# One encoder layer on one core: conditioning loads one pair of steps earlier, fewer conditioning steps beside the combination, and the fourth kind's softmax division done by the transposing product

## The chip, the core and the metric

The kernel runs on one core of a Trainium2 chip. The metric is the device time of one execution in microseconds (us), lower is better. Times, spans and waits below are from the runs of the kernel before and from the profile of one of its executions. Engines are named as the profile names them: PE is TensorE (PEld its weight loads), DVE is VectorE, ACT is ScalarE, POOL is GpSimd, SP is SyncE, which only issues transfers here.

## What is computed

One layer of an encoder trunk, for 1024 tokens of width 1024, all in float32. A conditioning vector c of width 1024 gives six modulation vectors; the layer is two residual blocks. The first has two attention branches: neighbourhood attention with 8 heads, and a mixture of three dilated windows with 4 heads each whose outputs are combined by their softmax denominators.

```python
mod = c_act @ w_ada[l] + b_ada[l]
sh1, sc1, gt1, sh2, sc2, gt2 = jnp.split(mod, 6, axis=-1)
h = rms_norm(x, g_norm1[l]) * (1.0 + sc1) + sh1
proj = h @ w_in[l]
qa, ka, va, qb, kb, vb, gates = jnp.split(proj, split_at, axis=-1)
o_a = neighbourhood_attention(rms_norm(qa), rms_norm(ka), va, rpb[l])
# three dilated windows on qb, kb, vb, combined by softmax of their log denominators
o_b = jnp.einsum('gbsh,gbshd->bshd', wts, jnp.stack(outs, axis=0))
merged = gate_a * (o_a @ w_proj_a[l]) + gate_b * (o_b @ w_proj_b[l])
x = x + gt1 * (merged @ w_o[l])
h2 = rms_norm(x, g_norm2[l]) * (1.0 + sc2) + sh2
a, up = jnp.split(h2 @ w_ffn_in[l], 2, axis=-1)
x = x + gt2 * ((jax.nn.silu(a) * up) @ w_ffn_out[l])
```

Inside `neighbourhood_attention` the scores get a bias, go through a softmax over at most 384 keys here, and the probabilities P multiply v.

## The kernel before

Every large product is made of three products of a high and a low part (`PASS`), so PE has most of the work. The program has these stages, by the time of the profiled execution: x is normalised and turned, and the first six blocks of tokens are projected (0 to 62 us); the combined projection with the attention worked in between (62 to 527); the first gate products with the last attention (527 to 616); the other gates, the merge, the output projection and the feed-forward part (616 to the end).

The projection is a loop over `n` from 6 to 91. `n = 8u + t`: `u` is one of ten units (a pair of heads: six of the dilated kinds 0, 1 and 2, then four of kind 3, the neighbourhood attention, which is "the fourth kind"), and `t` is a block of 128 tokens. Each `n` has eight chunks of three projection products on PE (line 305); between the fourth and the fifth chunk stand the scores of one item of attention, the product of P and v of an older one (line 510), the turns of q and k (line 370), and the turn of P of the item before (line 495). From `n = 58` on the items are those of kind 3, one for each `n`, until `n = 89`. An item of kind 3 has 128 queries, 2 heads and three blocks of 128 keys; the first and the last of a unit have two blocks.

For a head of kind 3, `at_qk` adds the bias to the scores and finds the negative maximum on DVE (line 483), takes the exponential and its sum on ACT (line 484), the reciprocal of the sum on DVE (line 486), and multiplies P by it on DVE (line 487). `at_turn`, one `n` later, transposes the blocks of P on PE into a PSUM bank with tag `t` (line 495) and copies the bank to SBUF, on ACT for the first head and on DVE for the second (lines 501 and 499). There are two banks of each tag.

The conditioning vectors that are needed late (4096 columns) are worked out beside all this: `ada_step` (line 278) is called once for an `n`, 65 times. A step multiplies a 128 by 512 piece of `w_ada` by one column of the activated c and adds it to `acc` on DVE (lines 292 and 294). The pieces are loaded in pairs, 512 KB at a time, by the step that uses the first of the pair (line 288), into a tile `wa` of the pool tag `big`. After eight steps `ada_row` (line 269) sums over the partitions with a product on PE into a bank `t` (line 271), adds the bias and stores the row; its two small tiles are of the tag `raw`.

`big` has eight tiles of 4 KB for a partition. They also hold v of a unit, the biases `rb` of kind 3, the pieces `tp`, the combination's sum `oacc` and more. `raw` has six tiles, into which all weights are loaded before they are split; the combination's `ut` and `fb` use them too. The combination of the three dilated kinds (`combine_step`) runs from `n = 64` (`COMB`) on: it turns the factors `fb` on PE into a bank `t` (line 665), and multiplies and adds on DVE (lines 673 to 676).

The order on PE is the order of the program. On DVE, ACT, POOL and SP a scheduler chooses the order when the program is built: it simulates the program and takes the first instruction in the program's order whose inputs are there by its simulation. In the built program each engine then runs its list strictly in order, so that an instruction that waits holds up all that stand behind it on its engine.

Of the kernel before, what the change touches and what calls it, by code (L numbers as in the profile page):

```python
# [10 lines left out]
F32 = mybir.dt.float32  # L11
F32R = mybir.dt.float32r
AF = mybir.ActivationFunctionType
ALU = mybir.AluOpType

S = 1024
# [7 lines left out]
NRAW, NHL = 6, 10  # L24
# [12 lines left out]
PAIRED, RBT, COMB = 58, 5, 64  # L37
# [6 lines left out]
def hybrid_layer(ctx: ExitStack, tc: tile.TileContext, x, colp, wada1, wada2, bada2, wqkv, wg, wpa, wpb,  # L44
                 wo, w1, w2, hgain, ropeg, rope, rbias, bmask, g2r, out):
    nc = tc.nc

    def pool(name, side, **kw):
        return tc.alloc_tile_pool(name=name, bufs=1, side=side, reuse_waits="tile", **kw)
# [4 lines left out]
    wp = pool("w", "left")  # L54
# [20 lines left out]
    def bank(tag):  # L75
        return ps.tile([128, 512], F32, tag=tag, name="ps_" + tag)
# [9 lines left out]
    ident = const.tile([128, 128], F32, name="ident")  # L86
# [5 lines left out]
    for i in (0, 2):  # L92
        nc.vector.scalar_tensor_tensor(hg[:, i:i + 1], hg[:, i:i + 1], 0.125, hg[:, i + 1:i + 2],
                                       op0=ALU.mult, op1=ALU.mult)
# [56 lines left out]
    def big(name, shape=None, dtype=F32):  # L151
        return ap_.tile(shape or wide, dtype, tag="big", bufs=NBIG, name=name)
# [27 lines left out]
    def unit_load(u, k):  # L180
        return wload(wqkv[u, :, k, :], 384)
# [84 lines left out]
    ada_state = {"i": 0}  # L266
    ada_acc = {}

    def ada_row(c):
        pm = bank("t")  # L270
        nc.tensor.matmul(pm[0:1, :], ones, ada_acc[c], start=True, stop=True)
        row = wp.tile([1, 512], F32, tag="raw", bufs=NRAW, name="row")
        br = wp.tile([1, 512], F32, tag="raw", bufs=NRAW, name="brow")
        nc.sync.dma_start(br, bada2[:, c * 512:(c + 1) * 512])
        nc.vector.tensor_add(row, pm[0:1, :], br)
        nc.sync.dma_start(mod_d[c * 512:(c + 1) * 512].rearrange("(o n) -> o n", o=1), row)

    def ada_step():
        i = ada_state["i"]
        ada_state["i"] += 1  # L280
        c, kk = divmod(i, 8)
        if kk == 0 and c > 0:
            ada_row(c - 1)
        if i >= 64:
            return
        if kk % 2 == 0:
            ada_acc["w"] = big("wa2", [128, 2, 512])
            nc.sync.dma_start(ada_acc["w"], wada2[c, :, kk:kk + 2, :])
        wa = ada_acc["w"][:, kk % 2, :]
        if kk == 0:  # L290
            ada_acc[c] = ap_.tile([128, 512], F32, tag="acc2", bufs=1, name="acc2")
            nc.vector.tensor_scalar(ada_acc[c], wa, cact[:, 0:1], None, op0=ALU.mult)
        else:
            nc.vector.scalar_tensor_tensor(ada_acc[c], wa, cact[:, kk:kk + 1], ada_acc[c],  # L294
                                           op0=ALU.mult, op1=ALU.add)
# [176 lines left out]
    @urgent(AQ)  # L472
    def at_qk(I, h):
        U, nq = I.U, I.nq
        nk = I.nkb * 128
        pS = I.pS[h]
        P = I.P[h] = ap_.tile([128, 512], F32, tag="p", bufs=4, name="P")
        if U.kind < 3:
            nm, sm = U.st[:nq, I.item, h:h + 1], U.st[:nq, I.item, 2 + h:3 + h]
        else:  # L480
            sx = ap_.tile([128, 3], F32, tag="sx", bufs=4, name="sx")
            nm, sm = sx[:nq, 0:1], sx[:nq, 1:2]
        nc.vector.tensor_tensor_reduce(P[:nq, :nk], pS[:nq, :nk], I.masks[h], -1.0, 3.0e38, ALU.add, ALU.min, nm)  # L483
        nc.scalar.activation(P[:nq, :nk], P[:nq, :nk], AF.Exp, scale=-1.0, bias=nm, accum_out=sm)  # L484
        if U.kind == 3:
            nc.vector.reciprocal(sx[:nq, 2:3], sm)
            nc.vector.tensor_scalar(P[:nq, :nk], P[:nq, :nk], sx[:nq, 2:3], None, op0=ALU.mult)

    @urgent(AT)
    def at_turn(I, h):  # L490
        nq, nkb = I.nq, I.nkb
        P = I.P[h]
        pt = bank("t")
        for i in range(nkb):
            nc.tensor.transpose(pt[:, i * 128:i * 128 + nq], P[:nq, i * 128:(i + 1) * 128], ident[:nq, :nq])
        PT = I.PT[h] = ap_.tile([128, 4, 128], F32, tag="pT", bufs=4, name="PT")
        src = pt.rearrange("p (b q) -> p b q", q=128)[:, :nkb, :nq]
        if h:
            nc.vector.tensor_copy(PT[:, :nkb, :nq], src)
        else:  # L500
            nc.scalar.activation(PT[:, :nkb, :nq], src, AF.Copy)
# [413 lines left out]
    for n in range(6, 92):  # L915
        u, t = divmod(n, 8)
        if u < 10:
            if t == 0:
                units.append(new_unit(u, [nextw[u, k] for k in range(KT)]))
            U = units[u]  # L920
            chunks = [lambda k=k, U=U, t=t: proj_chunk(U, t, k) for k in range(KT)]
        elif n - 80 < NPRE:
            chunks = gate_pre(n - 80)
        else:
            chunks = []
        if u + 1 < 10:
            for k in ([0, 1, 2, 3, 4, 5, 6, 7] if n == 6 else [t] if u else []):
                raws[u + 1, k] = unit_load(u + 1, k)
            if t == 6:
                for k in range(2):  # L930
                    nextw[u + 1, k] = wsplit(raws[u + 1, k])
        if t == 2 and 1 <= u <= 10:
            for slot, I in unit_items(units[u - 1]):
                if I.U.kind < 3:
                    waiting.append(I)
                else:
                    ready.setdefault(8 * u + 2 + slot, []).append(I)
        if n == 8 * 7 + 5:
            combine_stats()
        ci = n - COMB  # L940
        if 0 <= ci < 12:
            combine_prep(ci)
        if n >= PAIRED:
            done, prev, cur = prev, cur, ready.pop(n, [])
        elif n % 2:
            done, prev, cur = prev, cur, []
            if waiting:
                cur = [Cluster()]
                while waiting and cur[0].keys + waiting[0].nkb * 128 <= 512:
                    cur[0].add(waiting.pop(0))  # L950
        else:
            done = []

        def chunk():
            if chunks:
                chunks.pop(0)()
                k = 8 - len(chunks)
                if t == 7 and u + 1 < 10 and k < 8 and k >= 2:
                    nextw[u + 1, k] = wsplit(raws[u + 1, k], nc.vector if k % 2 else None)

        turns = [(units[0], tt) for tt in {8: (0, 1), 9: (2, 3), 11: (4, 5), 13: (6, 7)}.get(n, ())]
        if PAIRED <= n <= 81 or 9 < n < PAIRED and n % 2:
            turns += [(units[m // 8], m % 8) for m in ((n - 2,) if n >= PAIRED else (n - 3, n - 2)) if m >= 8]
        chunk()
        chunk()
        chunk()
        chunk()
        if n < 10:
            while chunks:
                chunk()  # L970
        if n >= PAIRED or n % 2 or n < 10:
            for I in cur:
                if I.__class__ is Cluster:
                    cl_scores(I)
                    cl_qk(I)
                else:
                    at_scores(I)
                    at_qk(I, 0)
                    at_qk(I, 1)
            for I in done:  # L980
                (cl_pv if I.__class__ is Cluster else at_pv)(I)
            for j in range(0, len(turns), 2):
                qk_turns(turns[j:j + 2], "s" if n < 10 else "v")
            for I in prev:
                if I.__class__ is Cluster:
                    cl_turn(I)
                else:
                    at_turn(I, 0)
                    at_turn(I, 1)
        chunk()  # L990
        chunk()
        chunk()
        chunk()
        if n >= 8 and (t != 7 or u > 8) and ada_state["i"] < 65:
            ada_step()
        if 2 <= u < 6 and t < 5:
            if t in (2, 4):
                t_piece(2 * (u - 2) + t // 2 - 1, 2)
            if t in (0, 2):
                t_piece(2 * (u - 2) + t // 2, 0)  # L1000
            if t in (1, 3):
                t_piece(2 * (u - 2) + t // 2, 1)
        if n in (85, 88):
            w1_combos((n - 85) // 3, EARLY[(n - 85) // 3])
        if 1 <= ci < 13:
            combine_step(ci - 1)
        while chunks:
            chunk()
        if u < 10:
            proj_post(U, t)  # L1010
            if U.kind == 3 and t == RBT:
                bias_tabs(U)
# [240 lines left out]
    for t in range(8):  # L1253
        pbs = [bank("dsv"[t % 3]) for _ in range(2)]
        ko = KFIRST if t == 0 else (KLAST if t == 7 else range(KT))
        for n, k in enumerate(ko):
            for hf in range(2):
                for a, b in PASS:
                    nc.tensor.matmul(pbs[hf], h2T[a][:, k, t * 128:(t + 1) * 128], wow[hf, k][b],  # L1259
                                     start=(n == 0 and (a, b) == PASS[0]), stop=(n == KT - 1 and (a, b) == PASS[2]))  # L1260
# [398 lines left out]
```

## Time and profile before

| | us |
|---|---|
| median of 3 runs | 1508.05 |
| lowest and highest run | 1505.69, 1510.28 |
| the profiled execution's own time | 1513.64 |
| its span, first to last instruction | 1511.8 |
| mean granted clock of TensorE | 0.997 of full speed |

The profile is read from the busy shares to the waits. An engine that is busy nearly all the time is a candidate for the bound; its idle time, and who ended it, tells what else costs time. A row of the list of waits reads: who waited, for whom, us in total, times, longest. A row of the timeline reads: start, length, engine, line, operation, result and inputs, size, count, and in brackets the idle time of the engine just before and what ended it. The records of PE overlap, because products are pipelined: the time that a product costs is read from the distance of two starts, not from the length of a record. A float32 product that is no transposition has two records.

### The profile page before, as it was taken

What the parts mean: (1) busy time and instruction counts of PE and PEld (TensorE: products, weight loads), DVE (VectorE), ACT (ScalarE), POOL (GpSimd) and SP (SyncE); (2) the same over time, 40 slices, a digit from 0 to 9 for tenths busy, and PEclk for the clock granted to TensorE, in tenths of its full rate; (3) what the DMA queues carried; (4) which work ended last, traced back from release to release, by engine and by line L of the source; (5) the groups of instructions that cost most, each with busy time, mean ns of one, the idle gap of its engine ahead of it and who ended that gap; (6) DMA issues with size and microseconds to landing.
All of it is one profiled execution on the core that took longest, in us unless ns stands there. A gap on an engine that the chain in (4) does not pass through costs nothing.

```text
span 1511.8 us, 24199 instructions
## 1 busy us (share of the span) xinstructions
PE 1486.6 (98%) x8156; PEld 1266.7 (84%) x8156; DVE 1087.9 (72%) x2265; ACT 669.9 (44%) x1691; POOL 535.6 (35%) x540
## 2 busy tenths in 40 slices
PE   8999999999999999999999999999999999999998
PEld 7999989998888877788888888888888888887886
DVE  6868777767888744466665497788767777599468
ACT  5656656555645554245532344233222333344442
POOL 0432333221100040001351311677767776104464
PEclk9999999999999999999999999999999999999999
DMA  9626444645235164833553235335433334798343
GB/s 365 232 80 190 144 145 145 190 137 166 76 114 176 47 192 135 308 106 123 176 178 143 87 96 182 119 132 180 157 130 105 109 108 146 269 366 288 99 150 103
DMA packets 150637, 241.65 MB, mean 160 GB/s; under 512 B 26464, under 2 KB 69088, under 8 KB 149744
## 3 DMA queue, kind: packets, MB, share of 16 engines
q1 hardware_dynamic: 131936, 226.45, 45.7%
q10 hardware_dynamic: 18576, 13.64, 2.8%
q8 instruction: 65, 1.06, 0.3%
q14 instruction: 60, 0.49, 0.1%
HBM read 179.89 MB, written 60.15 MB: 159 GB/s over the span
## 4 chain that ended last, share of the span: by engine, by line
PE 79%; DMA 8%; DVE 7%; ACT 3%; issue 2%; POOL 1%; SPq 0%; ACTq 0%; DVEq 0%
PE ps_d L305 11%; PE ps_v L1324 7%; PE ps_d L1324 7%; PE ps_s L1324 7%; PE ps_t L1324 6%; PE ps_d L705 4%; PE ps_s L1494 3%; PE ps_d L1494 3%; DMA wa<-in_wada_dram 3%; PE ps_v L1494 2%; PE ps_t L1494 2%; PE ps_s L1259 2%; PE ps_d L1259 2%; DVE wlo L119 2%; PE ps_v L1259 1%
## 5 line engine op out<-in xcount | busy, mean ns | idle before, releaser
L119 POOL TENSOR_TENSOR wlo<-raw,whi 128x512 fp32r<-128x512 f32 (+2 forms) x133 | 172.5, 1310 | 467.4 <-ACT whi L118 428.8
L118 ACT ACTIVATE whi<-raw 128x512 fp32r<-128x512 f32 (+1 forms) x348 | 203.9, 599 | 261.4 <-PE ps_s L1494 39.4
L305 PE MATMUL ps_d<-whi,hT 128*128 128x384 f32 x1152 | 312.0, 342 | 0.6 <-ACT vs L343 0.6
L119 DVE TENSOR_TENSOR wlo<-raw,whi 128x512 fp32r<-128x512 f32 (+1 forms) x215 | 181.9, 859 | 77.1 <-ACT whi L118 72.5
L305 PEld LDWEIGHTS ps_d<-whi,hT 128*128 128x128 f32 x1152 | 210.8, 189 | 6.1 <-ACT vs L343 4.4
L305 PE MATMUL ps_d<-wlo,hT 128*128 128x384 f32 x576 | 193.8, 337 | 2.4 <-DVE wlo L119 2.1
L305 PEld LDWEIGHTS ps_d<-wlo,hT 128*128 128x128 f32 x576 | 109.2, 190 | 3.1 <-DVE wlo L119 2.4
L118 ACT ACTIVATE whi<-ws 128x512 fp32r<-128x512 f32 x65 | 40.8, 628 | 128.2 <-DVE ws L1341 85.4
L1274 POOL TENSOR_TENSOR e<-e,c 128x512 f32<-128x512 f32 x44 | 68.8, 1563 | 61.0 <-DVE c L1404 36.8
L335 POOL TENSOR_TENSOR ra<-qn,rtab 128x64 f32<-128x64 f32 x48 | 16.2, 338 | 154.5 <-DVE qn L328 137.5
L119 POOL TENSOR_TENSOR wlo<-m,whi 128x512 fp32r<-128x512 f32 x35 | 51.3, 1477 | 54.2 <-ACT whi L118 54.2
L1272 ACT ACTIVATE e<-e 128x512 f32<-128x512 f32 x44 | 27.4, 630 | 85.2 <-DVE e L1407 58.1
L548 ACT ACTIVATE P<-P,st 128x256 f32<-128x256 f32 (+2 forms) x100 | 45.8, 459 | 36.9 <-DVE st L546 36.9
L705 PE MATMUL ps_d<-hT,whi 128*128 128x512 f32 x192 | 60.5, 397 | 0.0
L129 ACT ACTIVATE ry<-ss,eps 128x4 f32<-128x4 f32 (+1 forms) x88 | 26.3, 298 | 75.0 <-DVE ss L326 62.5
L1324 PE MATMUL ps_v<-h2T,whi 128*128 128x512 f32 x192 | 59.2, 389 | 0.0
L1324 PE MATMUL ps_s<-h2T,whi 128*128 128x512 f32 x192 | 59.1, 389 | 0.0
L294 DVE SCALAR_TENSOR_TENSOR acc<-wa,cact,acc 128x512 f32<-128x512 f32 x56 | 42.0, 750 | 21.0 <-DMA wa<-in_wada_dram 20.8
L484 ACT ACTIVATE P<-P,sx 128x384 f32<-128x384 f32 (+1 forms) x64 | 37.1, 581 | 44.9 <-DVE sx L483 44.7
L1324 PE MATMUL ps_d<-h2T,whi 128*128 128x512 f32 x184 | 56.7, 390 | 0.0
L119 DVE TENSOR_TENSOR wlo<-ws,whi 128x512 fp32r<-128x512 f32 x45 | 50.6, 1125 | 8.1 <-ACT whi L118 8.1
L1273 DVE TENSOR_TENSOR e<-e 128x512 f32<-128x512 f32 x44 | 42.5, 974 | 16.6 <-ACT e L1272 16.6
(445 smaller groups left out, 3956.9 us busy)
## 6 DMA issues: line engine op xcount, KB each, us to landing
raw<-in_w_dram SPq DMA_DIRECT2D x139, 256.0 KB
ga_d<-e SPq DMA_DIRECT2D x77, 256.0 KB
raw<-ga_d SPq DMA_DIRECT2D x77, 256.0 KB
wa<-in_wada_dram SPq DMA_DIRECT2D x32, 512.0 KB
raw<-in_wqkv_dram SPq DMA_DIRECT2D x80, 192.0 KB
m<-in_w_dram SPq DMA_DIRECT2D x44, 256.0 KB
raw<-in_wg_dram SPq DMA_DIRECT2D x42, 256.0 KB
xt<-in_x_dram SPq DMA_DIRECT2D x16, 512.0 KB
```

Of the source, the lines that this page charges most:

```text
L118: nc.scalar.activation(hi[:, :n], r, AF.Copy)
L119: (eng or nc.gpsimd).tensor_sub(lo[:, :n], r, fview(hi[:, :n]))
L294: nc.vector.scalar_tensor_tensor(ada_acc[c], wa, cact[:, kk:kk + 1], ada_acc[c], op0=ALU.mult, op1=ALU.add)
L305: nc.tensor.matmul(pd[:, :384], tok(a, k, t), U.w[k][b][:, :384], start=(k == 0 and i == 0), stop=(k == KT - 1 and i == 2))
L484: nc.scalar.activation(P[:nq, :nk], P[:nq, :nk], AF.Exp, scale=-1.0, bias=nm, accum_out=sm)
L548: nc.scalar.activation(C.P[h][:nq, c], C.P[h][:nq, c], AF.Exp, scale=-1.0, bias=nm, accum_out=sm)
L705: nc.tensor.matmul(st["p"], gw[i, br][j][a][:, kk * 128:(kk + 1) * 128], hT[b][:, k, hs], start=(k == 0 and q == 0), stop=(k == 7 and q == 2))
L1259: nc.tensor.matmul(pbs[hf], h2T[a][:, k, t * 128:(t + 1) * 128], wow[hf, k][b], start=(n == 0 and (a, b) == PASS[0]), stop=(n == KT - 1 an ...
L1273: nc.vector.tensor_mul(sg, sg, a)
L1274: nc.gpsimd.tensor_mul(sg, sg, up)
L1324: nc.tensor.matmul(pb, w[p][:, k * 128:(k + 1) * 128], b[q][:, k], start=(k == 0 and i == 0), stop=(k == 3 and i == 2))
L1494: nc.tensor.matmul(pb[m], o[0][a][:, m * 128:(m + 1) * 128], o[1][b], start=(k == 0 and i == 0), stop=(k == HT - 1 and i == 2))
```

## The change

Four edits, three in the conditioning and one in the attention of the fourth kind:

1. `ada_row` takes one tile of the tag `big` in place of two of the tag `raw`.
2. `ada_load` is new: a step that begins a pair issues the load of the next pair as well, so that a pair is loaded when the pair before it begins.
3. For `n` from 64 to 75 a step is called at each third `n` only (66, 69, 72, 75), and not at each `n`. The 65th call moves from `n = 80` to `n = 87`.
4. For kind 3, P is no longer multiplied by the reciprocal on DVE. ACT writes the identity matrix times the reciprocal into the free last 128 columns of the P tile, and PE multiplies each block of P by that diagonal matrix in place of transposing it: the result is the transposed block, divided.

```diff
@@ ada_row @@
-        row = wp.tile([1, 512], F32, tag="raw", bufs=NRAW, name="row")
-        br = wp.tile([1, 512], F32, tag="raw", bufs=NRAW, name="brow")
+        z = big("row", [1, S])
+        row, br = z[:, 0:512], z[:, 512:1024]
         nc.sync.dma_start(br, bada2[:, c * 512:(c + 1) * 512])
...
+    def ada_load(i):
+
+        if i < 64 and i not in ada_acc.setdefault("w", {}):
+            c, kk = divmod(i, 8)
+            ada_acc["w"][i] = big("wa2", [128, 2, 512])
+            nc.sync.dma_start(ada_acc["w"][i], wada2[c, :, kk:kk + 2, :])
@@ ada_step @@
         if kk % 2 == 0:
-            ada_acc["w"] = big("wa2", [128, 2, 512])
-            nc.sync.dma_start(ada_acc["w"], wada2[c, :, kk:kk + 2, :])
-        wa = ada_acc["w"][:, kk % 2, :]
+            ada_load(i)
+            ada_load(i + 2)
+        wa = ada_acc["w"][i - kk % 2][:, kk % 2, :]
@@ at_qk @@
             nc.vector.reciprocal(sx[:nq, 2:3], sm)
-            nc.vector.tensor_scalar(P[:nq, :nk], P[:nq, :nk], sx[:nq, 2:3], None, op0=ALU.mult)
+            nc.scalar.activation(P[:, 384:512], ident, AF.Identity, scale=sx[:, 2:3])
@@ at_turn @@
-            nc.tensor.transpose(pt[:, i * 128:i * 128 + nq], P[:nq, i * 128:(i + 1) * 128], ident[:nq, :nq])
+            if I.U.kind == 3:
+                nc.tensor.matmul(pt[:, i * 128:(i + 1) * 128], P[:, i * 128:(i + 1) * 128], P[:, 384:512],
+                                 start=True, stop=True)
+            else:
+                nc.tensor.transpose(pt[:, i * 128:i * 128 + nq], P[:nq, i * 128:(i + 1) * 128], ident[:nq, :nq])
@@ the loop over n @@
-        if n >= 8 and (t != 7 or u > 8) and ada_state["i"] < 65:
+        if n >= 8 and (n % 3 == 0 if COMB <= n < COMB + 12 else t != 7 or u > 8) and ada_state["i"] < 65:
             ada_step()
```

The lines of the kernel after are 7 or 8 higher from `at_qk` to `at_turn` and 11 higher behind them.

How the edits stand in the built program is shown at three places. The first is PE, at one `n` of kind 3 with three blocks, between the fourth and the fifth chunk of the projection. Before:

```order
L305 MATMUL ps_d<-whi,hT_406 128x384
L469 MATMUL ps_s<-qk 128x384 x6
L510 MATMUL ps_v<-PT,v 64x128 x6
L370 MATMUL ps_v<-ident,qn 128x128 x2
L495 MATMUL ps_t<-ident,P 128x128 x6
L305 MATMUL ps_d<-whi,hT_112 128x384
```

After:

```order
L312 MATMUL ps_d<-whi,hT_406 128x384
L476 MATMUL ps_s<-qk 128x384 x6
L521 MATMUL ps_v<-PT,v 64x128 x6
L377 MATMUL ps_v<-ident,qn 128x128 x2
L503 MATMUL ps_t<-P 128x128 x6
L312 MATMUL ps_d<-whi,hT_112 128x384
```

Nothing moves there: six transpositions become six products at the same place.

The second is DVE at `n = 65`, where the first conditioning steps of the combination stood. Before (L326 to L134 are the norm of q and k, L483 the scores, L499 the copy of the turned P, L394 and L395 the parts of q and k):

```order
L487 TENSOR_SCALAR P<-P,sx 128x384
L326 TENSOR_REDUCE ss_6135<-sq 128x4
L130 TENSOR_SCALAR rv<-ss_6135 128x4
L294 SCALAR_TENSOR_TENSOR acc_5905<-wa_6231,cact,acc_5905 128x512 x2
L132 TENSOR_TENSOR rz<-ry,rv 128x4
L483 ISA P,sx<-ps_s,rb 128x256
L483 ISA sx 128x1
L483 ISA P,sx<-ps_s,rb 128x256
```

After:

```order
L402 TENSOR_TENSOR qk<-ps_v,qk 128x2x64
L333 TENSOR_REDUCE ss_6130<-sq 128x4
L130 TENSOR_SCALAR rv<-ss_6130 128x4
L132 TENSOR_TENSOR rz<-ry,rv 128x4
L133 SCALAR_TENSOR_TENSOR rz<-rz,ry 128x4
L490 ISA P,sx<-ps_s,rb 128x256
L490 ISA sx 128x1
L490 ISA P,sx<-ps_s,rb 128x256
```

The two conditioning products and the multiplication of P are gone from this place.

The third is DVE at the beginning of kind 3 (`n = 57` and 58). Its first load `wa` stands at the same place of SP's list in both programs, just behind the load of v. Before:

```order
L134 SCALAR_TENSOR_TENSOR ry<-rz,ry 128x4
L328 TENSOR_TENSOR qn<-qn,ry 128x256
L294 SCALAR_TENSOR_TENSOR acc_5129<-wa_5344,cact,acc_5129 128x512
L394 SCALAR_TENSOR_TENSOR qk<-ps_v,hg,qk 128x4x64
L395 TENSOR_TENSOR qk<-ps_v,qk 128x4x64
```

After:

```order
L134 SCALAR_TENSOR_TENSOR ry<-rz,ry 128x4
L335 TENSOR_TENSOR qn<-qn,ry 128x256
L301 SCALAR_TENSOR_TENSOR acc_5126<-wa_5341,cact,acc_5126 128x512 x2
L401 SCALAR_TENSOR_TENSOR qk<-ps_v,hg,qk 128x4x64
L402 TENSOR_TENSOR qk<-ps_v,qk 128x4x64
```

Here the scheduler has moved the products of a later pair forward to the place of the earlier one, and two of them, not one, now stand ahead of the parts of q and k.

## The prediction

> **What bounds the kernel now.** I read the busy shares first, then the stages, then what PE waited for, and only then the single stalls.
>
> ```profile
> span 1511.8 us, 24199 instructions
> ...
> PE 1486.6 (98%) x8156; PEld 1266.7 (84%) x8156; DVE 1087.9 (72%) x2265; ACT 669.9 (44%) x1691; POOL 535.6 (35%) x540
> ...
> PE 79%; DMA 8%; DVE 7%; ACT 3%; issue 2%; POOL 1%; SPq 0%; ACTq 0%; DVEq 0%
> ```
>
> PE is busy for 98% of the span. The chain that ended last gives 8% to DMA and 7% to DVE, but a step of the chain can pass through an engine while PE had other work. What those waits really cost is PE's idle time, 25 us in all.
>
> ```profile
> core 0: us, PE busy (x) PEld busy (x) DVE busy (x) ACT busy (x) POOL busy (x), PEclk, DMA share, GB/s
> 62.00:370.00 308.00, 301.48 (x2164) 280.14 (x2163) 223.39 (x732) 181.17 (x635) 97.05 (x224) 1.00 0.48 149
> 370.00:527.00 157.00, 149.85 (x1064) 132.22 (x1063) 132.51 (x442) 84.88 (x296) 11.92 (x10) 0.98 0.34 105
> 527.00:616.00 89.00, 89.00 (x537) 69.42 (x537) 41.44 (x121) 38.57 (x102) 18.08 (x14) 1.00 0.54 163
> ```
>
> These are three stages: the dilated kinds (62 to 370), kind 3 beside the projection (370 to 527), and kind 3 beside the gates (527 to 616). The middle one has DVE at 132.5 of 157 us, and only there the granted clock (PEclk) falls under 1.00. In the last PE never stops. The change touches nothing behind 616. The list of PE's waits from 62 to 616 us:
>
> ```profile
> engine line waited for: us in total, times, longest us
> PE ps_t L665 <- DVE PT L499: 3.7, 2, 1.9
> PE ps_d L305 <- DVE wlo L119: 2.1, 1, 2.1
> PE ps_t L495 <- DVE oacc L676: 1.9, 1, 1.9
> PE ps_v L370 <- POOL qn L338: 1.8, 2, 1.0
> PE ps_s L469 <- DVE qk L395: 1.7, 1, 1.7
> PE ps_v L370 <- DVE qn L328: 1.0, 1, 1.0
> PE ps_d L305 <- ACT vs L343: 0.6, 1, 0.6
> PE ps_d L305 <- POOL wlo L119: 0.4, 1, 0.4
> PE ps_t L271 <- DVE PT L499: 0.4, 1, 0.4
> PE ps_t L665 <- ACT PT L501: 0.2, 1, 0.2
> ```
>
> These ten rows sum to 13.8 us. That is what the four edits can take away in waits, plus what the clock loses behind a wait (below). Everything they add to PE has to be paid out of that.
>
> **Edit 4 on PE: the cost.**
>
> ```profile
> 14.79 1.95 PE L232 MATMUL ps_d<-xd,xt 128*128 128x128 f32 x16
> 16.58 1.24 PE L234 MATMUL ps_v<-ident,xt 128*128 128x128 f32 x7
> ...
> 409.96 0.82 PE L495 MATMUL ps_t<-ident,P 128*128 128x128 f32 x6
> 410.54 0.42 PE L305 MATMUL ps_d<-whi,hT 128*128 128x384 f32 x1
> ...
> L495 PE MATMUL ps_t<-ident,P x176: 272/273/329, 375.6 to 610.2; 128*128 128x128 f32 x176
> ...
> L232 PE MATMUL ps_d<-xd,xt x32: 275/275/377, 9.2 to 16.5; 128*128 128x128 f32 x32
> ```
>
> Line 495 transposes 176 blocks with one record each (4 units x 2 heads x 22 blocks), and six records reach over 0.82 us; with a last record of 0.273 us the starts are (0.82 - 0.273) / 5 = 0.109 us apart. The kernel already has the operation that takes its place: line 232 multiplies blocks of x by a diagonal matrix, in float32. Its eight products of one tile have 16 records, two each, (1.95 - 0.275) / 15 = 0.112 us apart. So a product costs 0.223 us where a transposition costs 0.109, and the edit adds 176 x 0.114 = **20.1 us** to PE. It all stands on the path: in the three stages PE has no idle time but the waits above, and in the last (11 items, 60 blocks) none at all.
>
> The Trainium skill, "TensorE: Matmul & The Clock Gate", section "Terms", says that the transposing mode is 4x faster for FP32. By that a product would cost 0.436 us and the edit add 57.6 us; the rows of line 232 make it 2.05 times, and I go by them.
>
> **Edit 4 on DVE and ACT.**
>
> ```profile
> L487 DVE TENSOR_SCALAR P<-P,sx 128x384 f32<-128x384 f32 x48 | 23.4, 488 | 1.2
> ...
> L487 DVE TENSOR_SCALAR P<-P,sx 128x256 f32<-128x256 f32 x16 | 7.7, 489 | 0.1
> ...
> L343 ACT ACTIVATE vs<-ps_d 128x128 f32<-128x128 f32 x22 | 6.3, 285 | 0.0
> ...
> L548 ACT ACTIVATE P<-P,st 128x256 f32<-128x256 f32 x60 | 30.2, 504 | 22.3 <-DVE st L546 22.3
> ```
>
> DVE loses 64 instructions, 31.1 us. ACT gets 64 of 128x128; the trace has none from SBUF with a scale, and I bound it by the 285 ns of a plain copy of that size and the 504 ns of the exponential at twice the size: 18 to 32 us, of which I take 18, the same size. ACT is busy 84.9 + 38.6 of 246 us here, so it has room. The diagonal is ready some 3 us behind the scores, and its product comes one `n`, about 7 us, later. I cost it at nothing; if ACT were late by its own wait at each of the 32 items, 0.3 us each would be 10 us.
>
> **Edits 1 to 3: what they take away.** A load that comes late stops DVE, and all that stands behind it:
>
> ```profile
> 211.66 0.75 DVE L294 SCALAR_TENSOR_TENSOR acc<-wa,cact,acc 128x512 f32<-128x512 f32 x1 [1.94 <-DMA wa<-in_wada_dram]
> 214.33 0.44 PE L305 MATMUL ps_d<-wlo,hT 128*128 128x384 f32 x1 [2.06 <-DVE wlo L119]
> ...
> 366.70 0.75 DVE L294 SCALAR_TENSOR_TENSOR acc<-wa,cact,acc 128x512 f32<-128x512 f32 x1 [4.01 <-DMA wa<-in_wada_dram]
> 368.55 0.50 PE L469 MATMUL ps_s<-qk 64*128 64x256 f32 x4 [1.67 <-DVE qk L395]
> ...
> 417.33 1.54 DVE L294 SCALAR_TENSOR_TENSOR acc<-wa,cact,acc 128x512 f32<-128x512 f32 x2 [1.35 <-DMA wa<-in_wada_dram]
> 421.29 0.86 PE L665 MATMUL ps_t<-ident,fb 128*128 128x128 f32 x4 [1.84 <-DVE PT L499]
> ...
> 487.61 0.41 PE L495 MATMUL ps_t<-ident,P 128*128 128x128 f32 x2 [1.92 <-DVE oacc L676]
> 498.75 0.66 PE L665 MATMUL ps_t<-ident,fb 128*128 128x128 f32 x4 [1.86 <-DVE PT L499]
> ...
> 421.00:425.00 4.00, 3.71 (x14) 3.71 (x15) 3.54 (x13) 1.69 (x7) 0.00 (x0) 0.58 0.82 276
> ...
> 499.00:503.00 4.00, 4.00 (x20) 3.56 (x20) 3.76 (x12) 1.17 (x5) 0.00 (x0) 0.64 0.09 20
> 503.00:507.00 4.00, 4.00 (x33) 3.45 (x30) 2.78 (x11) 2.32 (x8) 0.00 (x0) 0.93 0.06 16
> ```
>
> Behind the stalls at 421 and 499 the clock falls for 3.4 us to one half: 4 x (1 - 0.58) = 1.7 us lost, and 4 x (0.36 + 0.07) = 1.7. The Trainium skill, same page, section "What's actually happening", gives one idle window of about 3.4 us as the condition for that. By that rule stalls of 1.9 us would cost no clock, and the result would be 2.6 us higher; the windows show that two of five such stalls did.
>
> Stall by stall, with the order of the changed program:
>
> - 214: no conditioning product stands near this `wlo` any more; the pair ahead of it is used a few `n` earlier, the next one a few `n` later than its load. All of 2.1 us goes.
> - 421: the two products at 417 are gone (second piece of the order in the section on the change). 1.84 + 1.7 = 3.5 us go.
> - 487: the products at 486 move behind 527. 1.9 us go.
> - 499: DVE waited there for ACT, and ACT for a gate weight. The two small tiles of `raw` no longer stand before that weight, but SP still waits for other `raw` tiles: half of 1.86 + 1.7, 1.8 us.
> - The waits of 0.4 (line 271) and 0.2 us (line 665) behind DVE's queue: 0.6 us go.
> - The first wait for `qn` (1.0 us, at 87) is behind a conditioning pair that moves: half, 0.5 us.
> - 368 stays: SP issues that load behind the load of v in both programs, and the scheduler, which believes the data to be there, moves a later pair to the same place. Two products now stand ahead of the parts of q and k: 0.8 us more (two took 1.54 us at 417, one 0.75).
> - The second wait for `qn`, and those for lines 328, 343 and 119 on POOL, stay.
>
> The eight products that move behind 527 cost nothing: DVE is busy for 41 of 89 us there, and 8 x 0.75 us fit. Two of their loads can come late behind the gate weights in SP's queue; behind the waiting product stands the scores' line 490, whose P is needed one `n` later, so that up to some 4 us are hidden.
>
> The sum: +20.1 - 2.1 - 3.5 - 1.9 - 1.8 - 0.6 - 0.5 + 0.8 = **+10.5 us**. The profiled execution's 1513.6 us would become 1524.1. It lies 5.6 us above the median of the runs, so I put the difference on the median: 1508.05 + 10.5 = **1518.5 us**.
>
> **The rivals.** A measurement of this kernel can tell about 0.3% (4.5 us) from no change.
>
> - *All waits go* (not slower). DVE loses 31 of its 174 us in the two stages with kind 3, and PE's longer turns give it 0.7 us more in each `n`. If this clears every wait from 62 to 616 us that DVE, ACT or POOL ends, 13.8 + 3.4 = 17.2 us go and 2.9 stay: 1511. It decides at the stall at 368 and the waits for `qn`. Against it: these stand in the first stage, where DVE's list hardly changes.
> - *The loads stay late.* The scheduler uses each product as early as its simulation allows, so that an earlier load is followed by an earlier use, as at 368. If this happens wherever a pair moved, only edit 4's lighter DVE helps, and 1 to 4 us of the gain are left: 1508 + 20.1 - 2.5 = 1526.
> - *A new wait.* The diagonal on ACT is late (10 us, above), or a load blocks SP before the gate weights: +5 to +10 on top of the forecast, 1526.
> - *The doubled pass is hidden.* If PE's second record ran beside other products, the cost would vanish and only the gains count: 1508 - 9.6 = 1498. Against it: line 232's records follow each other without overlap of starts, and PE is full.
> - *Four transpositions' time for a product.* 176 x 3 x 0.109 = 57.6 us instead of 20.1, less the 9.6 gained: 1556. Line 232's 0.223 us speaks against it. This is the result of the first rule of the Trainium skill above.
>
> **How the numbers follow.** The forecast with its own spread (1514 to 1523, where the halves of the two doubtful stalls go all one way or the other and a stall or two more stays or goes) has 62%; all waits go 13%; the loads stay late 14%; a new wait 8%; the pass hidden 2%; four times 1%. The range from 1511 to 1528 takes in the forecast, the late loads, the smaller new waits and half of the case in which all waits go, some 8 in 10. Slower by over 0.3% (above 1512.6): 62 + 14 + 8 + 1 = 85%, and 1% of the case of all waits gone, 86%. Within 0.3%: 12%. Faster: the hidden pass, 2%.
>
> **What would show it.** On PE, line 503 has two records for each block, 0.112 us apart, and 352 in all; a group of three blocks and two heads takes about 1.3 us where six transpositions took 0.58 (409.96 to 410.54). From 527 to 616, where nothing else changes for PE, the stage becomes 60 x 0.114 = 6.8 us longer. The clock stays at 1.00 near 421, the wait at 214 is gone, that at 368 is there and a little longer. It would be wrong if PE's idle time from 62 to 616 stayed near 14 us, or if one record for a block were found.

## The result and the profile after

The changed kernel takes **1529.56 us**, the median of four runs (1528.24 to 1530.77). The kernel before, measured beside it, has 1507.91 (1505.69 to 1510.28). The ratio is 1.014, with a 95% interval from 1.0124 to 1.0155: slower by 21.65 us. The forecast was 1518.5 with a range up to 1528, so the direction was right, and the rise was twice as large as forecast.

The profiled execution of after took 1530.77 us, 17.2 more than that of before. The busy shares and the shares of the chain that ended last:

```profile
span 1529.0 us, 24591 instructions
...
PE 1507.7 (99%) x8332; PEld 1287.1 (84%) x8332; DVE 1070.7 (70%) x2201; ACT 686.5 (45%) x1755; POOL 536.6 (35%) x540
...
PE 83%; DMA 7%; DVE 5%; issue 2%; ACT 1%; POOL 1%; SPq 1%; ACTq 0%; DVEq 0%; POOLq 0%
```

Two subtractions split the 17.2 us. PE is busy for 1507.7 - 1486.6 = 21.1 us more. It is idle for 1529.0 - 1507.7 = 21.3 us where it was idle for 25.2, so only 3.9 us less. The stages, cut where the same work ends, and the two stretches of low clock:

```profile
core 0: us, PE busy (x) PEld busy (x) DVE busy (x) ACT busy (x) POOL busy (x), PEclk, DMA share, GB/s
62.00:376.00 314.00, 304.39 (x2161) 282.57 (x2161) 225.92 (x734) 180.85 (x635) 96.81 (x223) 0.99 0.47 147
376.00:537.00 161.00, 160.27 (x1184) 143.75 (x1183) 114.57 (x388) 100.11 (x345) 16.61 (x14) 1.00 0.35 106
537.00:633.00 96.00, 96.00 (x590) 75.75 (x588) 39.75 (x108) 41.82 (x117) 13.27 (x10) 1.00 0.47 138
147.00:151.00 4.00, 4.00 (x17) 3.41 (x17) 3.10 (x16) 2.87 (x12) 1.07 (x4) 0.59 1.02 344
219.00:223.00 4.00, 4.00 (x22) 3.53 (x21) 2.18 (x10) 1.09 (x5) 2.14 (x8) 0.57 0.86 255
```

In the second stage the idle time fell from 157 - 149.85 = 7.2 us to 0.7, and the clock is back at 1.00. In the first stage it rose from 308 - 301.48 = 6.5 us to 9.6, and both stretches of half clock now lie there. What PE waited for from 62 to 633 us:

```profile
PE ps_d L312 <- DVE wlo L119: 3.7, 2, 2.7
PE ps_v L377 <- POOL qn L345: 2.7, 2, 1.5
PE ps_s L476 <- DVE qk L402: 1.8, 1, 1.8
PE ps_v L377 <- DVE rz L132: 1.2, 1, 1.2
PE ps_t L676 <- ACT PT L512: 0.5, 1, 0.5
```

All but the last row belong to the first stage, which was to become shorter. Behind them stand the conditioning loads. This is DVE's row for them after (us, times, longest):

```profile
DVE acc L301 <- DMA wa<-in_wada_dram: 22.9, 9, 4.1
```

And before:

```profile
DVE acc L294 <- DMA wa<-in_wada_dram: 20.8, 13, 5.4
```

So in these two executions the loads issued a pair ahead are waited for as long as before. Three places of the timeline of after:

```profile
141.69 0.75 DVE L301 SCALAR_TENSOR_TENSOR acc<-wa,cact,acc 128x512 f32<-128x512 f32 x1 [1.56 <-DMA wa<-in_wada_dram]
146.86 0.44 PE L377 MATMUL ps_v<-ident,qn 128*128 128x128 f32 x2 [1.46 <-POOL qn L345]
...
212.96 1.54 DVE L757 TENSOR_TENSOR tp<-tp 128x512 f32<-128x512 f32 x1 [1.97 <-DMA tp<-h_d]
218.03 0.44 PE L312 MATMUL ps_d<-wlo,hT 128*128 128x384 f32 x1 [2.66 <-DVE wlo L119]
...
371.83 1.54 DVE L301 SCALAR_TENSOR_TENSOR acc<-wa,cact,acc 128x512 f32<-128x512 f32 x2 [4.07 <-DMA wa<-in_wada_dram]
374.50 0.51 PE L476 MATMUL ps_s<-qk 64*128 64x256 f32 x4 [1.75 <-DVE qk L402]
```

The first stall is new: four products stand among the norm of q and k, the first of them waits, and `qn` is late. At 218 the stall of 214 has another origin: DVE no longer waits for `wa` there, but for the next load in its list, `tp`. The third is the stall at 368.

### The profile page after: what moved, and what is told of

It reads as the page before. It is cut to its first block, busy times and chain, and to the rows that moved or that the text cites. A ratio compares the mean times of both kernels' runs of the same rounds, so it can differ in the third digit from the quotient of the medians.

```text
span 1529.0 us, 24591 instructions
## 1 busy us (share of the span) xinstructions
PE 1507.7 (99%) x8332; PEld 1287.1 (84%) x8332; DVE 1070.7 (70%) x2201; ACT 686.5 (45%) x1755; POOL 536.6 (35%) x540
## 4 chain that ended last, share of the span: by engine, by line
PE 83%; DMA 7%; DVE 5%; issue 2%; ACT 1%; POOL 1%; SPq 1%; ACTq 0%; DVEq 0%; POOLq 0%
PE ps_d L312 14%; PE ps_v L1335 7%; PE ps_d L1335 7%; PE ps_s L1335 7%; PE ps_t L1335 6%; PE ps_d L716 4%; PE ps_v L1505 3%; PE ps_t L1505 3%; PE ps_s L1505 3%; PE ps_d L1505 3%; PE ps_t L503 2%; PE ps_s L1270 2%; PE ps_d L1270 2%; DMA wa<-in_wada_dram 2%; PE ps_v L1270 1%
## 5 line engine op out<-in xcount | busy, mean ns | idle before, releaser
L1284 DVE TENSOR_TENSOR e<-e 128x512 f32<-128x512 f32 x44 | 42.5, 973 | 17.2 <-ACT e L1283 17.1
```

The lines of the kernel that those rows point to most:

```text
L1284: nc.vector.tensor_mul(sg, sg, a)
```

## The experiments

Eleven kernels, and the kernel before once more for a second profile. The first four of the table were measured beside 19 runs of the kernel before (median 1508.3), the others beside 15 and 11 (median 1509.2 both times). Costs below are differences from the median of the same group. "Idle" is PE's idle time from 60 to 640 us in the profiled execution, summed over the gaps of its records.

| run | us, median | ratio to before, 95% | idle, us |
|---|---|---|---|
| edit4_alone | 1526.89 | 1.0116 (1.0091 to 1.0141) | 8.3 |
| edits123_alone | 1512.68 | 1.0026 (1.0008 to 1.0044) | 13.3 |
| product_by_identity | 1529.07 | 1.0127 (1.0106 to 1.0147) | 8.5 |
| p_scaled_on_act | 1506.66 | 0.9975 (0.9960 to 0.9990) | 10.3 |
| edit2_alone | 1507.60 | 0.9990 (0.9978 to 1.0001) | 9.9 |
| edit3_alone | 1517.56 | 1.0053 (1.0041 to 1.0066) | 14.7 |
| after_products_pinned | 1518.30 | 1.0061 (1.0048 to 1.0075) | 0.7 |
| before_again | 1511.01, one run | | 11.0 |
| before_pinned | 1497.07 | 0.9923 (0.9906 to 0.9940) | 1.6 |
| edit2_pinned | 1495.77 | 0.9914 (0.9897 to 0.9932) | 1.5 |
| edits123_pinned | 1500.86 | 0.9948 (0.9930 to 0.9966) | 4.7 |
| edits123_act_pinned | 1496.39 | 0.9920 (0.9904 to 0.9937) | 1.7 |

The kernel before has 14.5 us of such idle time in its profiled execution, the kernel after 10.3.

### Edit 4 and edits 1 to 3 apart

The first run has edit 4 on the kernel before and nothing else; the second has edits 1 to 3 as in the diff above, without edit 4.

> The kernel before with edit 4 alone (P divided in its turn by the diagonal matrix). Theory A (the doubled products of edit 4 cost their full 20.1 us on PE, and edits 1 to 3 bring nothing, since the loads stay late): 1508 + 20.1 less at most 5 for the lighter DVE, 1523 to 1528. Theory B (edits 1 to 3 cost some 6 us by themselves, in the first stage, and edit 4 some 14): 1519 to 1523.

> The kernel after without edit 4 (P is multiplied on DVE and transposed, as before). Theory A: within 0.3% of before, 1504 to 1512, and DVE's wait for the conditioning loads stays near 21 us. Theory B: 1512 to 1516, with the loss between 62 and 370 us.

They cost 18.6 and 4.4 us, together 23.0, where the whole change costs 21.65. So the two halves nearly add up, edit 4 is by far the larger, and edits 1 to 3 do not pay anything back: as a group they cost. That is theory A for edit 4, and the time of theory B for the rest. The place of theory B fits only in part: at 350 us, aligned by PE's instructions, the profile of edits123_alone is 0.4 us behind that of before, and behind the stall at 368 (2.4 us there, and 6.8 us at half clock) it is 4.1.

### The diagonal product's price

Here the product by a matrix replaces the transposition, but the matrix is the plain identity and DVE still scales P:

```diff
             if I.U.kind == 3:
-                nc.tensor.matmul(pt[...], P[...], P[:, 384:512], start=True, stop=True)
+                nc.tensor.matmul(pt[...], P[...], ident, start=True, stop=True)
```

> The kernel before, but the blocks of P of the fourth kind are multiplied by the identity matrix as float32 products where they were transposed; DVE still multiplies P. This is the cost on PE alone. Theory A: 176 x 0.114 = 20.1 us, with nothing for a lighter DVE, 1526 to 1530. If the doubled products fill PE's waits instead, 1518 to 1523.

20.8 us for PE's part alone, where the prediction's sum had 20.1. The groups of after say the same: a row of the timeline with two heads of three blocks, and the two rows of the groups for the product and for the diagonal on ACT:

```profile
418.12 1.50 PE L503 MATMUL ps_t<-P 128*128 128x128 f32 x12
...
L503 PE MATMUL ps_t<-P 128*128 128x128 f32 x352 | 45.7, 278 | 0.1
...
L494 ACT ACTIVATE P<-ident,sx 128x128 f32<-128x128 f32 x64 | 24.5, 394 | 5.7 <-DVE sx L493 5.6
```

Twelve records for six blocks, (1.50 - 0.275) / 11 = 0.111 us apart, 352 in all. The relief of DVE is worth 20.8 - 18.6 = 2.2 us, a difference that lies within the two intervals. ACT pays 24.5 us, where the prediction took 18 of a range from 18 to 32; that it costs nothing on the path was right: PE is idle for only 0.1 us in all ahead of line 503, and no wait of PE ends with line 494.

The same relief is to be had without the product, when ACT scales P in place:

```diff
-            nc.vector.tensor_scalar(P[:nq, :nk], P[:nq, :nk], sx[:nq, 2:3], None, op0=ALU.mult)
+            nc.scalar.activation(P[:nq, :nk], P[:nq, :nk], AF.Copy, scale=sx[:nq, 2:3])
```

> The kernel before, but P of the fourth kind is multiplied by the reciprocal on ACT, in place, and transposed as before: DVE loses the 31 us, PE gains nothing. Theory A (DVE's load matters little by itself, the waits for loads do): 1504 to 1509. If DVE's load makes the waits at 421 and 499 us: 1498 to 1503.

1.6 us faster than before. So taking the scaling off DVE is worth about 2 us (clear of noise here, though small), and the 20 us are the price of the place to which edit 4 moved it.

### Edits 2 and 3 apart, and a second profile of before

> Only edit 2 of the change (a pair of conditioning blocks loaded one pair ahead), on the kernel before. The order of DVE's instructions in the first stage is then the changed kernel's: the products stand in runs of three and four where they stood in pairs. Theory C (the scheduler uses the earlier load at once, so the lead is spent in the order): the products run close behind their loads as before, DVE's waits for them stay at 14 to 23 us, and the whole price of edits 1 to 3 is here: 1510 to 1514 us. Theory D (the price comes from edit 3, which puts the products later, or from edit 1, whose row tile takes a big buffer): 1506 to 1509 us here.

> Only edit 3 (conditioning steps at every third n between 64 and 75), on the kernel before; the first 370 us keep their order. Theory C: 1505 to 1509 us, the stall near 421 us shorter or gone and nothing else moved. Theory D: 1510 to 1514 us.

> The kernel before, unchanged, for a second profile: how much of PE's lost time before 616 us is the same from one execution to the next. The profile shown has 1513.6 us against a median of 1508. If its stalls at 421 and 499 us, with half the clock behind them, belong to that execution alone, this one shows fewer and some 1506 to 1509 us; if they are always there, 1512 to 1514.

Theory C missed on the price: edit 2 costs nothing (its interval holds 1), and **edit 3 costs 8.3 us**, more than theory D allowed it. DVE's waits for the loads are 13.4 us with edit 2 alone, just under what C gave, so the lead did not remove them. Edit 1 was not tried alone. Why edit 3 costs: it does take the stalls at 421, 487 and 499 away (0.7 and 0.3 us at line 665 are left), but the last two rows of modulation are summed at 516 and 583 instead of 473 and 536, among the gate weights. PE's and SP's timelines and SP's waits there, in edit3_alone:

```profile
582.78 1.02 PE L271 MATMUL ps_t<-acc,ones 128*1 128x512 f32 x2
588.50 1.22 PE L705 MATMUL ps_d<-hT,whi 128*128 128x512 f32 x2 [4.70 <-ACT whi L118]
...
519.18 2.75 SPq L111 DMA_DIRECT2D raw<-in_wg_dram  x6
...
575.82 8.11 SPq L712 DMA_DIRECT2D sig_d<-gsig  x2
584.02 0.38 SPq L111 DMA_DIRECT2D raw<-in_wg_dram  x1
...
SPq L712 <- ACT gsig L711: 20.3, 4, 7.4
```

SP's list carries the row's transfers, the results of the gates and the gate weights. The weight that PE waits for was issued at 584.02, behind a store of `gsig` for which SP waited 7.4 us; PE stood for 4.7 us, and the clock was at half for 6.8 us. From 515 to 613 us PE has four waits, 8.8 us in all, where before has none of such length.

SP issued no gate weight for 62 us, from 521.6 to 584.0; in edits123_alone, which has edits 1 and 2 as well, it issued thirteen in that time. Edit 1 takes the row's two tiles out of `raw`, into which the gate weights are loaded, so the gap may come from those tiles. Edits 1 and 3 without edit 2 were not run, so this is not shown.

With edits 1 and 2 beside it (edits123_alone) that stall is gone and another has come. Behind 519 us, POOL's, DVE's and PE's rows:

```profile
519.63 10.48 POOL L119 TENSOR_TENSOR wlo<-raw,whi 128x512 fp32r<-128x512 f32 x8 [23.16 <-ACT whi L118]
...
522.22 1.21 DVE L133 SCALAR_TENSOR_TENSOR rz<-rz,ry 128x4 f32<-128x4 f32 x1
523.46 1.22 DVE L134 SCALAR_TENSOR_TENSOR ry<-rz,ry 128x4 f32<-128x4 f32 x1
524.61 1.50 DVE L494 TENSOR_SCALAR P<-P,sx 128x384 f32<-128x384 f32 x1
526.03 1.48 DVE L335 TENSOR_TENSOR qn<-qn,ry 128x256 f32<-128x256 f32 x1
...
528.03 1.86 PE L271 MATMUL ps_t<-acc,ones 128*1 128x512 f32 x2 [3.14 <-DVE PT L506]
```

The row's sum needs a bank `t`, the bank waits for DVE's copy `PT`, and the copy stands behind four operations that take 1.2 to 1.5 us each. Over this profile the median of line 134 is 0.16 us and that of line 494 (128x384) 0.42. POOL splits weights at the same time, 1.3 us each, and each of the four ends within 0.3 us of the end of one of them, so it seems to wait for it. The Trainium skill, "SBUF — State Buffer", section "SBUF: two separate sides", says that DVE and GpSimd share one pair of ports under an exclusive lock, held for a whole instruction; on DVE's side it names operations with two inputs in SBUF, against a GpSimd operation that reads SBUF, and operations in a two-port mode. By that, four operations would be held by up to four splits, and the rows agree: 5.4 us for four, where four splits take 5.2. Lines 133, 134 and 335 have two such inputs; line 494 has one and a factor, and no trace shows its mode. In the changed kernel the scaling of line 494 is no longer there, and PE does not wait at this place. So part of edit 4's relief seems to be that it clears a stall which edit 3 makes; the pinned runs below bear this out.

The second profile of before has these waits of PE from 62 to 616 us, among others:

```profile
PE ps_t L665 <- DVE PT L499: 4.2, 2, 2.5
PE ps_d L305 <- DVE wlo L119: 2.0, 1, 2.0
...
PE ps_t L495 <- DVE oacc L676: 0.4, 1, 0.4
...
PE ps_s L469 <- DVE qk L395: 0.4, 1, 0.4
```

The stalls at 214, 421 and 499 recur, 2.0, 2.5 and 1.7 us. That at 487 is 0.4 where the first profile has 1.9, that at 368 is 0.4 where it has 1.7, and one stretch of half clock is left of two. PE's idle time is 3.5 us less (14.5 and 11.0), the half clock 1.7. The time, 1511.01, lies between the two forecasts. The first profile thus showed more than this execution lost, and this one is still 1.8 us above the median.

### The order of the products

The scheduler puts a product where its simulation has the data. The next run keeps the change and fixes the 64 products in the order of the program; `pin` is the kernel's own name for the framework's way to do so.

```diff
-            nc.vector.tensor_scalar(ada_acc[c], wa, cact[:, 0:1], None, op0=ALU.mult)
+            pin(nc.vector.tensor_scalar(ada_acc[c], wa, cact[:, 0:1], None, op0=ALU.mult))
...
-            nc.vector.scalar_tensor_tensor(ada_acc[c], wa, ..., op0=ALU.mult, op1=ALU.add)
+            pin(nc.vector.scalar_tensor_tensor(ada_acc[c], wa, ..., op0=ALU.mult, op1=ALU.add))
```

> The changed kernel with the 64 conditioning products held in the order of the program, so that the scheduler can't move them up to the load: they then stand one every fifteen or so DVE instructions, evenly, with their loads a pair ahead. Theory C: DVE's waits for conditioning loads fall from 22.9 us to under 4, the stalls of PE at 147 and 218 us go, and the time falls by the 4 to 6 us of the first stage, to 1522 to 1527 us. The rival (the loads are late because SP issues them late or the transfers are slow, whatever the order): the waits stay over 12 us and the time at 1527 to 1533.

11.3 us less than the changed kernel, twice what theory C asked for. DVE waits for no conditioning load any more. PE's waits from 62 to 633 us, all of them, and the stages:

```profile
PE ps_v L377 <- POOL qn L345: 0.4, 1, 0.4
PE ps_d L312 <- DVE wlo L119: 0.2, 1, 0.2
...
62.00:376.00 314.00, 313.39 (x2252) 291.61 (x2251) 234.00 (x773) 191.17 (x670) 104.31 (x223) 1.00 0.48 148
376.00:537.00 161.00, 160.87 (x1186) 142.67 (x1185) 115.89 (x372) 97.94 (x332) 22.69 (x19) 1.00 0.39 117
537.00:633.00 96.00, 96.00 (x566) 76.55 (x565) 37.41 (x95) 38.83 (x102) 6.90 (x6) 1.00 0.52 158
```

The trace also gives the lead itself: from the start of each of the 32 issues on SP to the first product that uses the load. In the profiled executions its median is 7.1 us before, 9.6 after, and 26.8 in the pinned changed kernel; 24 of 32 leads are under 9 us before, 14 after, none pinned. A load takes about as long as that: the one waited for at 141.69 was issued 7.3 us earlier. So the scheduler gave most of the new lead away, by moving the products up to the loads.

Four more kernels ask whether the lead or the order matters, and what edit 3 and the scaling are worth when the products are pinned: the kernel before with `pin` alone; with edit 2; with edits 1 to 3; and the last with P scaled in place on ACT.

> The kernel before, with the 64 conditioning products held in program order and nothing else (its loads are issued at their own step, not a pair ahead). Theory O (the order is all: the scheduler puts the products in runs close behind their loads, and spread evenly they collide with nothing): DVE's waits for conditioning loads under 5 us in all, PE idle from 60 to 640 us under 4 us where the two profiles of before have 14.5 and 11.0, and 1497 to 1502 us. Theory L (the lead is needed as well): the waits stay over 10 us, the idle time over 6 us, and 1503 to 1510 us.

> Edit 2 alone with the products pinned: loads a pair ahead and the even order. Both theories: DVE waits for no conditioning load, PE idle from 60 to 640 us under 2 us, 1495 to 1500 us. Against before_pinned it gives the worth of the lead by itself: nothing by theory O, 5 us or more by theory L.

> The changed kernel without edit 4, with the products pinned. It was 1512.7 us unpinned and the changed kernel is 1518.3 pinned, so if edit 4 costs its 20 us here too, 1497 to 1500 us; and if edit 3 is harmful by itself (fewer steps beside the combination push work behind 527 us) it stands 4 us or more above edit2_pinned, if only through the scheduler's early products, level with it.

> The same with the fourth kind's P scaled on ACT in place in stead of on DVE: no diagonal product, DVE's 64 scalings gone, PE without its 176 records. With PE idle already under 2 us before 640 there is nothing left for DVE's relief to save: level with edits123_pinned within 1.5 us, 1495 to 1500 us. If DVE's scalings still hold PE up somewhere, 2 us or more below it.

The order alone gives 12.1 us (before_pinned), and the lead at most some 1.3 more (edit2_pinned; the runs of the two overlap): theory O, though its bound on DVE's waits was missed (6.9 us are left, which cost PE little: it is idle for 1.6 us). Holding the products also makes the scheduler place others anew: of the 2201 other instructions of DVE, 1890 keep their order from before to before_pinned. So the 12.1 us are the worth of the new order as a whole. **edit2_pinned beats both kernels**, at 1495.77 us:

```profile
span 1494.5 us, 24203 instructions
...
62.00:370.00 308.00, 308.00 (x2212) 287.47 (x2211) 231.92 (x765) 187.97 (x656) 104.72 (x223) 1.00 0.48 151
370.00:527.00 157.00, 155.60 (x1118) 134.65 (x1117) 132.03 (x435) 85.38 (x295) 13.41 (x12) 1.00 0.37 115
```

PE has no idle time left in the first stage. Edits 1 and 3 cost 5.1 us on top, pinned too; in the profile 3.1 of them are the stall of line 271 at 512, the same as at 528 above. With P scaled on ACT it shrinks to 1.1, and the time falls by 4.5 us, so DVE's scalings did hold PE up there; that expectation's premise, PE idle for under 2 us, was off (4.7). Edit 4, added to the pinned edits 1 to 3, costs 1518.30 - 1500.86 = 17.4 us.

With the products pinned in both, the whole change costs 1518.30 - 1497.07 = 21.2 us, as much as without (21.65): pinning takes 12.1 us from the kernel before and 11.3 from the changed one. So what the order of the products loses, the change leaves nearly whole.

## Why the prediction was too low

The step that failed is the credit of 9.6 us for edits 1 to 3 ("what they take away"). As a group they take nothing away: they cost 4.4 us alone, and 1529.56 - 1526.89 = 2.7 on top of edit 4. The terms that came out the other way are those of the first stage. Term by term, from the two profiled executions:

- **Edit 4 on PE, +20.1.** Right: 20.8 us alone, 21.1 us more busy time in the profile.
- **421, 487 and 499, and line 665.** Right in direction and too careful: the idle time of 376 to 537 us is 0.7 us, and all of these stalls went, the doubtful half too; 0.5 us at line 676 is left. Edit 3 alone removes them nearly as well.
- **The last stage, +6.8.** From the first gate product to the first of line 724 (735 after) it is 7.4 us longer (91.4 to 98.9), and 7.3 with edit 4 alone. That the moved products cost nothing held in the changed kernel, where PE has no idle time in this stage; with edit 3 alone and with edits 1 to 3 it did not (4.7 us at 588, 3.1 at 528).
- **214, and the first `qn`: wrong.** "No conditioning product stands near this `wlo` any more ... All of 2.1 us goes" followed one product out of DVE's list and didn't ask what stands there in its place. It was a load of `tp` (1.97 us), and the stall grew to 2.7. In all nine profiles without pinned products it stays (1.6 to 2.7 us), and in all five with them it is gone. The first wait for `qn` did not halve but went from 1.0 to 1.2, and three more stalls came, at 147, 286 and 364 (1.5, 1.3 and 1.0 us). The prediction's sum has for the first stage -2.1 - 0.5 + 0.8 = -1.8 us; measured are 9.6 - 6.5 = +3.1 of idle time and two stretches of half clock, 1.7 us each: 8.3 us off. The size is that of this execution, the direction is not: idle time and half clock (counted with the stall ahead of it) together lose 4.3 to 6.7 us in this stage in the six unpinned profiles without edit 2, and 7.4, 10.6 and 13.0 in the three with it (edit2_alone, edits123_alone, after). The median of edit2_alone is no longer for it, so edit 2 must win as much back elsewhere; where, was not followed.
- **368 stays.** Right, but it grew by 0.1 us (1.67 to 1.75), not by 0.8.
- **Against which execution.** The sum took its credits from the profiled execution and put them on the median, 5.6 us lower. An execution near the median doesn't have all of these stalls to give (the second profile has 5.2 us less of them): the medians differ by 21.65 us, the profiled executions by 17.2. That is the other 4.4 us of the miss.

Together: the forecast's 10.5 + 1.0 (edit 4) + 8.3 (first stage) - 2.0 (second stage: idle time and clock give 9.8 where 7.8 were forecast) - 0.6 (the rest of the idle time) = 17.2 us, the difference of the two profiles.

The rival nearest to what happened is *the loads stay late* (1526): its mechanism, an earlier load followed by an earlier use, is shown by the leads and by the pinned runs. It had no price for the first stage, so it too was low. *All waits go* came true in its waits, not in its time, with the products pinned: 0.7 us of idle time, but 1518.30 us where it had 1511, since the pinning was worth 11.3 us in the median, and the rival took 17.2 off the forecast's 20.1.

What stays open: up to the end of the first stage the built programs of the changed kernel and of edits123_alone are the same on DVE, ACT and POOL. Yet at 350 us, aligned by PE's instructions, the one profile is 4.6 us behind before and the other 0.4. So the order makes these stalls possible; what decides how many of them come in an execution, perhaps when the transfers land, was not settled.

## What to carry to other kernels

A prefetch under a scheduler is worth only the lead that remains between issue and first use in the built order, so count that lead in the trace, and try a fixed order of the uses before adding buffers. When a stall's cause is moved away, look at what moves into its place in the same strict queue. Credits for stalls should come from more than one profiled execution, because a median run may not have them.

## What the runs showed of the chip

Stalls of PE of nearly the same length sometimes cost clock and sometimes not: 1.46 us at 147 in the changed kernel was followed by 3.41 us at half clock, 1.75 us at 374 was not, and 3.12 us at 512 in edits123_pinned was not. The stretches behind a stall last 3.41 us or twice that. The Trainium skill, "TensorE: Matmul & The Clock Gate", section "What's actually happening", has windows of 3413 ns that run freely. The length agrees, and with free windows it would matter where a stall falls, which no run here tests; but its condition of one idle window was not needed here, since a stall of less than half a window was enough.
